# A hybrid stream-encoder layer: token tiles 0 to 3 transposed by TensorE instead of by DMA, their loads and the f weights' issued earlier

## The chip, the cores and the metric

The kernel runs on one core of a Trainium2 chip. The core has five engines with an instruction queue each: TensorE (PE; its weight loads are shown apart as PEld), VectorE (DVE), ScalarE (ACT), GpSimd (POOL) and SyncE (SP), which here issues nearly all DMAs. The metric is the device time of one execution in microseconds (us), less is better.

## The reference, cut to what matters

The input x has 2048 tokens of 1024 channels in float32. One layer is computed:

```python
h = _rmsnorm(x, pre_norm_g[l])
proj = jnp.einsum('btd,de->bte', h, w_in[l])
q_a, f_a, i_a, g_a, u_b, g_b, q_c, k_c, v_c, g_c, f_c = jnp.split(proj, IN_SPLIT_POINTS, axis=-1)
...
o_a = _hgrn2_chunkwise(jax.nn.silu(q_a).reshape(hshape), k_a.reshape(hshape),
                       i_a.reshape(B, T, HGRN_HEADS, HGRN_VAL_DIM), log_f_a.reshape(hshape))
...
pooled = _multiscale_pool(u_b)
...
o_c = _forgetting_attention(q_c.reshape(fshape), k_c.reshape(fshape), v_c.reshape(fshape), log_f_c)
...
mixed = jnp.concatenate([o_a, o_b, o_c], axis=-1)
y = jnp.einsum('bte,ed->btd', mixed, w_out[l])
x = x + _rmsnorm(y, post_norm_g[l])
```

A is a gated linear recurrence (4 heads, 64x64 state; its inputs are q_a, f_a and i_a, 256 columns of the projection each), B a pooling mixer, C a forgetting attention with 8 heads. The input projection has 3592 columns over a depth of 1024.

## The kernel before

**Tiles.** The tokens are cut into 16 tiles of 128 (partitions), and these into 4 groups of 512. Every factor of the projection is split into two float16 halves, high and low, and a product takes three matmuls (high with high, low with high, high with low). The normalised tokens are kept transposed, channels on the partitions: hTh and hTl, high and low halves, 8 blocks of 128 channels.

**A token tile** is made by `x_parts` (L208), a generator which its caller advances with `next`: the load xt (SP), a Square with a sum on ACT (L213), mean and epsilon into ss on DVE (L214), the power -1/2 on POOL (L217, "pow" below), xh on ACT (L218, the tile scaled by ss, as float16), xl on DVE (L220, what xh leaves over), and two DMA transposes on SP, xh into hTh (L221) and xl into hTl (L223). xt, ss, xh and xl have two buffers each.

**Weights** come through `w_parts` (L138): 256 columns in four quarters of two depth blocks, a load into a staging tile wst (three buffers; the weights for i are staged in four others), and for each block a high half wh (L161 on ACT, for i on POOL) and a low half wl (L164 on DVE). The eight columns of the attention's gate stand in wfc (L482 to L484) and are projected together with i.

**The start phase** (L465 to L509) is written out by hand, and `sp()` keeps its instructions in program order (`ordered[0]`, until L509): the loads of tile 0, of the weights for i and of tile 1, tiles 0 to 3 with the halves of i between them, the quarters of f, and the i projection of tiles 0 and 1 (`tok_i`, L235: pi on TensorE, evicted by ACT into va, L239, and fcs, L240). Behind it the library's scheduler chooses each engine's order from what is recorded. Next in the program come the weights q, tiles 4 and 5, and the constants on POOL (masks, d0, zeros; L538 to L583), which `tc.issue_after` puts behind the pow of tile 5. Then the first `hgrn_f` and `hgrn_q` (the projections pf and pq over a group of 512 tokens, and the elementwise work behind them: E, z, b, khat, qhat), the weights k, tiles 6 and 7, and the loads of x8 and x9. The later tiles are fed in between the levels of the recurrence's units (`feed`); there each level makes an X (POOL or DVE, then ACT) and a Z, and TensorE multiplies them; khT (L335) is a transposed khat that pu (L368) needs.

**The rest** is eight such units (4 groups, 2 channel halves), then the projections of the other parts, the attention over blocks of 128 queries, and the output projection.

Of the kernel before, what the change touches and what calls it, by code (L numbers as in the profile page):

```python
# [10 lines left out]
F16 = mybir.dt.float16  # L11
# [4 lines left out]
AF = mybir.ActivationFunctionType  # L16
ALU = mybir.AluOpType
# [5 lines left out]
P = 128  # L23
NT = T // P
KC = D // P
# [29 lines left out]
def kernel(  # L55
# [7 lines left out]
    V, S, G, PE = nc.vector, nc.scalar, nc.gpsimd, nc.tensor  # L63
# [6 lines left out]
    cp = ctx.enter_context(tc.tile_pool(name="cp", bufs=1))  # L70
# [5 lines left out]

    idf = cp.tile([P, P], F32, tag="idf", name="idf")
    make_identity(nc, idf)
    cneg = cp.tile([P, 8], F32, tag="cneg", name="cneg")
    G.memset(cneg, -0.5)  # L80

# [27 lines left out]
    psA = phP.enter_context(tc.tile_pool(name="psA", bufs=1, space=PSUM, reuse_waits="tile"))  # L109
# [7 lines left out]
    def h_at(t0, n):  # L117
        i, o = divmod(t0, T // 2)
        return hTs[i][0][:, :, o:o + n], hTs[i][1][:, :, o:o + n]
# [9 lines left out]
    def sp(ins):  # L129

        if ordered[0]:
            tc.keep_in_program_order(ins)
        return ins
# [3 lines left out]
    def w_parts(segs, name, pool=None, hi_eng=None, stage=None, extra=0):  # L137
        n = sum(w for _, w in segs)  # L138
        pool = pool or wpool
        wh = pool.tile([P, KC, n + extra], F16, tag="wh", name=f"wh_{name}")  # L140
        wl = pool.tile([P, KC, n + extra], F16, tag="wl", name=f"wl_{name}")
        staged = {}

        def load(q):
            if stage:
                st = stage(f"wst_{name}_{q}").rearrange("p (k n) -> p k n", k=WK)
            else:
                st = wpool.tile([P, WK, n], F32, tag="wst", name=f"wst_{name}_{q}", bufs=3)
            o = 0
            for c0, w in segs:  # L150
                sp(nc.sync.dma_start(st[:, :, o:o + w],
                                     win[q * WK * P:(q + 1) * WK * P, c0:c0 + w].rearrange("(k p) c -> p k c", p=P)))
                o += w
            staged[q] = st

        def halves(q):
            st = staged.pop(q)
            for kk in range(WK):
                k = q * WK + kk
                if hi_eng is None:  # L160
                    sp(S.activation(wh[:, k, :n], st[:, kk, :], AF.Copy, bias=0.0, scale=g256[:, k:k + 1]))  # L161
                else:
                    sp(hi_eng.tensor_scalar(wh[:, k, :n], st[:, kk, :], g256[:, k:k + 1], 1.0, op0=ALU.mult, op1=ALU.mult))
                sp(V.scalar_tensor_tensor(wl[:, k, :n], st[:, kk, :], g256[:, k:k + 1], wh[:, k, :n],  # L164
                                          op0=ALU.mult, op1=ALU.subtract))

        return (wh, wl), load, halves
# [28 lines left out]

    last_pow = [None]

    xts = {}
    def x_dma(xpool, t, tag="xt"):  # L200
        xt = (xpool if tag == "xt" else ap).tile([P, D], F32, tag=tag, name=f"xt{t}", bufs=2)
        sp(nc.sync.dma_start(xt, xf[t * P:(t + 1) * P, :]))
        xts[t] = xt

    def x_parts(xpool, t, tag="xt"):
        if t not in xts:
            x_dma(xpool, t, tag)
        xt = xts.pop(t)  # L208
        ss = xpool.tile([P, 4], F32, tag="ss", name=f"ss{t}", bufs=2)
        xh = xpool.tile([P, D], F16, tag="xh", name=f"xh{t}", bufs=2)  # L210
        xl = xpool.tile([P, D], F16, tag="xl", name=f"xl{t}", bufs=2)
        hh, hl = h_at(t * P, P)
        sp(S.activation(xh.bitcast(BF16), xt, AF.Square, bias=0.0, scale=1.0, accum_out=ss[:, 0:1]))  # L213
        sp(V.tensor_scalar(ss[:, 1:2], ss[:, 0:1], 1.0 / (D * SH * SH), EPS / (SH * SH),  # L214
                           op0=ALU.mult, op1=ALU.add))
        yield
        last_pow[0] = sp(G.tensor_tensor(ss[:, 2:3], ss[:, 1:2], cneg[:, 0:1], op=ALU.pow))  # L217
        sp(S.activation(xh, xt, AF.Copy, bias=0.0, scale=ss[:, 2:3]))  # L218
        yield
        sp(V.scalar_tensor_tensor(xl, xt, ss[:, 2:3], xh, op0=ALU.mult, op1=ALU.subtract))  # L220
        sp(nc.sync.dma_start_transpose(hh, xh))  # L221
        yield
        sp(nc.sync.dma_start_transpose(hl, xl))  # L223

    def x_load(xpool, t, tag="xt"):
        for _ in x_parts(xpool, t, tag):
            pass
# [7 lines left out]
    def tok_i(t, wi, va):  # L235
        tt = t % 4
        pi = pj(f"pi{t}")
        proj_tm(pi[:, :264], wi, 0, 264, t)
        sp(S.activation(va[:, tt, :], pi[:, :256], AF.Copy, bias=0.0, scale=INV))  # L239
        sp(S.activation(fcs[:, t, :], pi[:, 256:264], AF.Copy, bias=0.0, scale=INV))  # L240
# [217 lines left out]
    xpool = xstk.enter_context(tc.tile_pool(name="xpool", bufs=2, side="right", reuse_waits="tile"))  # L458
# [7 lines left out]
    wi, load, halves = w_parts([(IA, 256)], "i", hi_eng=G, stage=tmp, extra=8)  # L466
# [3 lines left out]
    wfc = t512("X", "wfc", 4)[:, :8 * KC].rearrange("p (k c) -> p k c", k=KC)  # L470
    sp(nc.sync.dma_start(wfc, win[:, FC:FC + 8].rearrange("(k p) c -> p k c", p=P)))
    x_dma(xpool, 1, "at")
    x0, x1, x2, x3 = (x_parts(xpool, t) for t in range(4))
    next(x0)
    next(x0)
    halves(0)
    next(x0)
    x_dma(xpool, 2, "at")
    next(x0, None)
    x_dma(xpool, 3)  # L480
    halves(1)
    sp(V.tensor_tensor(wfc, wfc, g256.unsqueeze(2).to_broadcast([P, KC, 8]), op=ALU.mult))  # L482
    sp(V.tensor_copy(wi[0][:, :, 256:264], wfc))
# [2 lines left out]
    halves(2)  # L486
    halves(3)
    next(x1)
    next(x1)
    next(x1, None)  # L490
    wf, load, halves = w_parts([(FA, 256)], "f")
    next(x2)
    next(x2)
    next(x2)
    next(x2, None)
    for q in range(3):
        load(q)
    tok_i(0, wi, toks[0])
    next(x3)
    next(x3)  # L500
    next(x3)
    next(x3, None)
# [55 lines left out]
    G.affine_select(out=mdiag, in_=mdiag, pattern=[[1, P]], compare_op=ALU.is_ge,  # L558
                    fill=0.0, base=0, channel_multiplier=-1)

    idh = cp.tile([P, P], F16, tag="idh", name="idh")
    V.tensor_copy(idh, idf)
    idb = cp.tile([P, P], BF16, tag="idb", name="idb")
    V.tensor_copy(idb, idf)

# [30 lines left out]
    def feed():  # L596

        for t in range(8, NT):
            parts = x_parts(xpool, t)
            for k in range(3):  # L600
                next(parts)
                if k < 2:
                    yield
            next(parts, None)
            if t + 2 < NT:
                x_dma(xpool, t + 2)
            yield
# [595 lines left out]
```

## Time and profile before

| | |
|---|---|
| runs | 1254.1, 1251.9, 1248.07 us; median 1251.9 |
| the profiled execution | 1248.18 us, of which the span that the trace shows is 1246.4 |
| granted TensorE clock, mean | 0.987 |
| TensorE matmul / weight load busy | 1170.5 us (94%) / 749.9 (60%) |
| DVE / ACT / POOL busy | 812.2 (65%) / 609.5 (49%) / 403.7 (32%) |
| DMA | 107.56 MB, mean 86 GB/s |

How to read a row of the profile. A row of the timeline has the start in us, the duration, the engine, the line, the operation, the tile written and those read (buffer numbers are left out, so xh is the xh of any token tile), the shape of output and input, and, in brackets, the idle time of that engine just before and what ended it. x2 or x4 behind it means so many in a row, with the time of all. A row of the windows has the stretch, its length, then busy time and count of PE, PEld, DVE, ACT and POOL, then the granted clock, the DMA share and GB/s. The 40 slices show busy tenths in equal parts of the span (31 us each).

### The profile page before, as it was taken

The page shows a single profiled execution, that of the slowest core. Times are in us where ns is not written, and L with a number is a line of the kernel's source. Part 1 is how long each engine was busy: PE and PEld are TensorE (multiplying, and loading weights), DVE is VectorE, ACT ScalarE, POOL GpSimd, SP SyncE. Part 2 cuts the span into 40 slices and gives each one's busy share as a digit, 9 for nine tenths or more (in the row PEclk, how much of TensorE's full clock was granted, in tenths as well). Part 3 has the DMA queues.
Part 4 walks back from the last instruction along what each step waited for, and adds up shares of the span by engine and source line. Part 5 has one row for each costly group of instructions (what it writes and reads, how often), then busy time and mean ns, then how long its engine had stood idle before and what let it go on. Part 6 is the DMA issues. An engine that isn't in the chain of part 4 may idle for free.

```text
span 1246.4 us, 25487 instructions
## 1 busy us (share of the span) xinstructions
PE 1170.5 (94%) x9949; PEld 749.9 (60%) x9949; DVE 812.2 (65%) x1736; ACT 609.5 (49%) x1176; POOL 403.7 (32%) x500
## 2 busy tenths in 40 slices
PE   5877999999999999999999999999989899999998
PEld 3445667655644588884447767755555555555544
DVE  5787878887433243214364799788788888888522
ACT  5756444553121222212122677667767676777611
POOL 2645555553130020002230223234334343434400
PEclk9988999999999999999999999999999999999999
DMA  9646100113175232101112343285223222321263
GB/s 226 184 115 170 44 17 18 52 35 93 43 183 142 71 107 71 35 2 43 26 51 70 89 140 110 69 178 127 67 64 85 68 78 79 65 51 38 80 162 104
DMA packets 168137, 107.56 MB, mean 86 GB/s; under 512 B 95824, under 2 KB 159568, under 8 KB 168016
## 3 DMA queue, kind: packets, MB, share of 16 engines
q1 hardware_dynamic: 166976, 105.92, 32.2%
q8 instruction: 78, 1.28, 0.4%
q14 instruction: 43, 0.35, 0.1%
q10 hardware_dynamic: 1040, 0.00, 0.0%
HBM read 59.62 MB, written 31.59 MB: 73 GB/s over the span
## 4 chain that ended last, share of the span: by engine, by line
PE 62%; DVE 19%; ACT 6%; issue 5%; POOL 4%; DMA 4%; SPq 0%; POOLq 0%; DVEq 0%; ACTq 0%
PE y L1078 11%; PE pq L183 7%; PE pv L194 6%; PE pgc L194 5%; PE pu L183 3%; PE st L1009 3%; PE st L1010 3%; PE pgb L183 3%; PE pk L183 3%; DVE pl L1024 3%; PE mx L973 3%; DVE M L979 3%; PE o L1034 2%; PE o L1035 2%; PE pf L183 2%
## 5 line engine op out<-in xcount | busy, mean ns | idle before, releaser
L1019 ACT ACTIVATE pf<-st,biasg 128x512 f32<-128x512 f32 (+1 forms) x320 | 199.6, 625 | 93.9 <-PE st L1010 53.2
L194 PEld LDWEIGHTS <-hTh 128*128 128x128 f16 x1536 | 151.0, 99 | 44.3 <-DMA hTh<-xh 16.1
L1024 DVE TENSOR_TENSOR pl<-pf,ph 128x512 f16<-128x512 f32 (+1 forms) x213 | 139.9, 658 | 42.4 <-POOL ph L1021 24.8
L1024 POOL TENSOR_TENSOR pl<-pf,ph 128x512 f16<-128x512 f32 (+2 forms) x107 | 114.2, 1067 | 147.7 <-ACT ph L1023 137.6
L979 DVE TENSOR_REDUCE M<-mx 128x1 f32<-128x512 f32 x192 | 129.2, 682 | 9.4 <-PE mx L973 8.5
L1023 ACT ACTIVATE ph<-st,biasg 128x512 f16<-128x512 f32 (+2 forms) x213 | 131.4, 617 | 2.1 <-PE o L1036 2.1
L1034 PE MATMUL o<-Vt,ph 128*128 128x65 f16 x1088 | 129.7, 193 | 2.8 <-DVE oc L1048 2.4
L1035 PE MATMUL o<-Vt,ph 128*128 128x64 f16 x1088 | 130.2, 195 | 0.0
L1036 PE MATMUL o<-Vt,pl 128*128 128x65 f16 x1088 | 129.2, 192 | 0.0
L1021 POOL TENSOR_SCALAR ph<-pf 128x512 f16<-128x512 f32 (+1 forms) x107 | 66.0, 617 | 192.4 <-ACT pf L1019 130.8
L1034 PEld LDWEIGHTS <-ph 128*128 128x128 f16 x1088 | 102.6, 96 | 34.5 <-issue 5.5
L1009 PE MATMUL st<-QQ,K 128*128 128x512 f16 (+1 forms) x320 | 111.5, 349 | 5.6 <-ACT ph L1023 5.0
L1035 PEld LDWEIGHTS <-ph 128*128 128x128 f16 x1088 | 101.8, 97 | 24.5 <-issue 1.1
L1036 PEld LDWEIGHTS <-pl 128*128 128x128 f16 x1088 | 102.3, 99 | 0.4
L1078 PE MATMUL y<-woh,mh 128*128 128x512 f16 (+2 forms) x264 | 98.2, 373 | 0.0
L1078 PE MATMUL y<-woh,ml 128*128 128x512 f16 (+2 forms) x264 | 98.0, 373 | 0.0
L1078 PE MATMUL y<-wol,mh 128*128 128x512 f16 (+2 forms) x264 | 98.0, 373 | 0.0
L973 PE MATMUL mx<-KA,QM 68*128 68x512 f16 (+1 forms) x224 | 79.5, 358 | 5.7 <-DVE M L979 4.1
L194 PEld LDWEIGHTS <-hTl 128*128 128x128 f16 x768 | 75.5, 98 | 9.9
L1010 PE MATMUL st<-QB,KA 68*128 68x512 f16 x224 | 80.1, 358 | 0.0
L1078 PEld LDWEIGHTS <-mh 128*128 128x128 f16 x528 | 49.4, 98 | 50.4 <-issue 0.7
L976 DVE CUSTOM_DVE_ANT_0 mx<-mx,negq 128x128 f32<-128x128 f32 (+3 forms) x128 | 62.3, 492 | 12.0 <-PE mx L973 11.5
(327 smaller groups left out, 2691.1 us busy)
## 6 DMA issues: line engine op xcount, KB each, us to landing
xt<-in_x_dram SPq DMA_DIRECT2D x16, 512.0 KB, 4.4
xr<-in_x_dram SPq DMA_DIRECT2D x16, 512.0 KB, 4.5
out_dram<-yt SPq DMA_DIRECT2D x15, 512.0 KB, 3.1
QQ<-qh_d SPq DMA_DIRECT2D x64, 64.0 KB, 2.3
wo<-in_w_out_dram SPq DMA_DIRECT2D x16, 256.0 KB, 3.0
gc_d<-gtc SPq DMA_DIRECT2D x32, 128.0 KB, 2.0
gtl<-gc_d SPq DMA_DIRECT2D x16, 256.0 KB, 2.9
wst_q<-in_w_in_dram SPq DMA_DIRECT2D x12, 256.0 KB, 2.9
```

What stands on the lines that cost most here:

```text
L183: PE.matmul(ps, a[:, k, c0:c0 + P], b[:, k, :], start=i == 0, stop=i == 3 * KC - 1)
L194: PE.matmul(ps, a[:, k, :], b[:, k, c0:c0 + n], start=i == 0, stop=i == 3 * KC - 1)
L979: V.tensor_reduce(dst, mx[:, :w], op=ALU.max, axis=AX.X)
L1009: PE.matmul(st[:, off:], K2[c][:, h, jj * P:(jj + 1) * P], QQs[i][:, off:], start=True, stop=False)
L1010: PE.matmul(st[:, off:], KA[c][:68, h, jj * P:(jj + 1) * P], QBs[i][:68, off:], start=False, stop=not diag)
L1019: S.activation(pf[:, off:], st[:, off:], AF.Exp, bias=bias, scale=0.125)
L1023: S.activation(ph[:, off:], st[:, off:], AF.Exp, bias=bias, scale=0.125)
L1024: (G if k == 1 else V).tensor_tensor(pl[:, off:], pf[:, off:], ph[:, off:], op=ALU.subtract)
L1034: PE.matmul(pov[:, qi, :], ph[:, qs], Vt[:, j, h, 0:65], start=(j == 0 and qi == 0), stop=False, skip_group_check=True)
L1035: PE.matmul(pov[:, qi, 0:64], ph[:, qs], Vt[:, j, h, 65:129], start=False, stop=False, skip_group_check=True)
L1036: PE.matmul(pov[:, qi, :], pl[:, qs], Vt[:, j, h, 0:65], start=False, stop=(j == 4 * g + qi), skip_group_check=True)
L1078: PE.matmul(py, a[:, k, :], b[:, k, cs], start=i == 0, stop=i == 3 * KC - 1)
```

## The change

An identity in float16, idh, is made at the very start instead of behind the constants. For tiles 0 to 3 `x_parts` makes no DMA transposes any more: `pe_transposed` has TensorE transpose the eight 128x128 blocks of xh into a PSUM bank (tag pm, one of six), and ACT copies them into hTh; xl goes the same way, and DVE copies it into hTl. These tiles now take one `next` less. The loads of x2 and x3 and of the first three f quarters stand further ahead in the program.

```diff
+    idh = cp.tile([P, P], F16, tag="idh", name="idh")
+    V.tensor_copy(idh, idf)
...
+    def pe_transposed(src, name):
+        pt = psA.tile([P, KC, P], F16, tag="pm", name=name, bufs=6)
+        for k in range(KC):
+            PE.transpose(pt[:, k, :], src[:, k * P:(k + 1) * P], idh)
+        return pt
...
         last_pow[0] = sp(G.tensor_tensor(ss[:, 2:3], ss[:, 1:2], cneg[:, 0:1], op=ALU.pow))
         sp(S.activation(xh, xt, AF.Copy, bias=0.0, scale=ss[:, 2:3]))
+        if t < 4:
+
+            sp(S.activation(hh, pe_transposed(xh, f"xhT{t}"), AF.Copy, bias=0.0, scale=1.0))
+            yield
+            sp(V.scalar_tensor_tensor(xl, xt, ss[:, 2:3], xh, op0=ALU.mult, op1=ALU.subtract))
+            sp(V.tensor_copy(hl, pe_transposed(xl, f"xlT{t}")))
+            return
         yield
...
     x_dma(xpool, 1, "at")
+    x_dma(xpool, 2, "at")
+    x_dma(xpool, 3)
     x0, x1, x2, x3 = (x_parts(xpool, t) for t in range(4))
     next(x0)
     next(x0)
     halves(0)
-    next(x0)
-    x_dma(xpool, 2, "at")
     next(x0, None)
-    x_dma(xpool, 3)
     halves(1)
...
     halves(3)
     next(x1)
-    next(x1)
     next(x1, None)
     wf, load, halves = w_parts([(FA, 256)], "f")
-    next(x2)
+    for q in range(3):
+        load(q)
     next(x2)
     next(x2)
     next(x2, None)
-    for q in range(3):
-        load(q)
     tok_i(0, wi, toks[0])
-    next(x3)
     next(x3)
     next(x3)
     next(x3, None)
...
-    idh = cp.tile([P, P], F16, tag="idh", name="idh")
-    V.tensor_copy(idh, idf)
```

The order of the engines' rows before the first unit and in it is another one; further on the rows of ACT, DVE, POOL, SP and TensorE are the same again. TensorE has 128 rows more (64 transposes and their weight loads), ACT and DVE four each, SP eight fewer. In the rows that follow, a number behind a name tells buffers apart; names like xh6 carry the token tile.

DVE before, behind xl of tile 0 (L164 are low halves of i, L482 to L484 the gate columns, L214 the ss of tile 1):

```order
L220 SCALAR_TENSOR_TENSOR xl0_129<-xt0_111,ss0_127,xh0_128 128x1024
L164 SCALAR_TENSOR_TENSOR wl_i_114<-wst_i_1_117,g256_69,wh_i_113 128x256 x2
L482 TENSOR_TENSOR wfc_123<-wfc_123,g256_69 128x64
L516 TENSOR_TENSOR lb_e_326<-lbt_324 128x2
L483 CAST wh_i_113<-wfc_123 128x8x8
L484 TENSOR_TENSOR wl_i_114<-wfc_123,wh_i_113 128x8x8
L214 TENSOR_SCALAR ss1_152<-ss1_152 128x1
```

DVE of the change at the same place:

```order
L231 SCALAR_TENSOR_TENSOR xl0_135<-xt0_113,ss0_133,xh0_134 128x1024
L232 COPY hTl0_100<-xlT0_155 128x8x128
L166 SCALAR_TENSOR_TENSOR wl_i_116<-wst_i_1_119,g256_71,wh_i_115 128x256 x2
L496 TENSOR_TENSOR wfc_125<-wfc_125,g256_71 128x64
L497 CAST wh_i_115<-wfc_125 128x8x8
L498 TENSOR_TENSOR wl_i_116<-wfc_125,wh_i_115 128x8x8
L222 TENSOR_SCALAR ss1_172<-ss1_172 128x1
```

The copy of xlT0 out of PSUM now stands between xl0 and all that follows it.

ACT before, from the q halves (wh_q) to the first elementwise row of hgrn_f (E):

```order
L161 ACTIVATE wh_q_341<-wst_q_1_349,g256_69 128x256 x2
L213 ACTIVATE xh5_382,ss5_381<-xt5_379 128x1024
L218 ACTIVATE xh5_382<-xt5_379,ss5_381 128x1024
L161 ACTIVATE wh_q_341<-wst_q_2_355,g256_69 128x256 x2
L161 ACTIVATE wh_q_341<-wst_q_3_361,g256_69 128x256 x2
L254 ACTIVATE E_0_0_486<-pf_0_0_460 128x512
```

ACT of the change, from the Square of tile 5 (L221) to the same row:

```order
L221 ACTIVATE xh5_456,ss5_455<-xt5_453 128x1024
L221 ACTIVATE xh6_651,ss6_650<-xt6_648 128x1024
L163 ACTIVATE wh_f_208<-wst_f_3_303,g256_71 128x256 x2
L254 ACTIVATE va0_112<-pi3_371 128x256
L255 ACTIVATE fcs_74<-pi3_371 128x8
L163 ACTIVATE wh_q_415<-wst_q_0_417,g256_71 128x256 x2
L163 ACTIVATE wh_q_415<-wst_q_1_423,g256_71 128x256 x2
L226 ACTIVATE xh5_456<-xt5_453,ss5_455 128x1024
L226 ACTIVATE xh6_651<-xt6_648,ss6_650 128x1024
L163 ACTIVATE wh_q_415<-wst_q_2_429,g256_71 128x256 x2
L163 ACTIVATE wh_q_415<-wst_q_3_435,g256_71 128x256 x2
L269 ACTIVATE E_0_0_558<-pf_0_0_532 128x512
```

The Squares of tiles 5 and 6 have moved ahead of the last f halves, and xh of tile 6 (L226) ahead of the last q halves. On POOL the pow of tile 6, which xh6 needs, stands behind the constants, before and now.

ACT before, in the first unit (khat L287, X of two levels L350, E and z of the second channel half):

```order
L287 ACTIVATE khat_0_0_509<-khat_0_0_509 128x512
L350 ACTIVATE X_0_0_64_729<-X_0_0_64_729 128x512
L350 ACTIVATE X_0_0_32_746<-X_0_0_32_746 128x512
L254 ACTIVATE E_0_1_774<-pf_0_1_604 128x512
L255 ACTIVATE z_0_1_773<-pf_0_1_604 128x512
```

ACT of the change there:

```order
L365 ACTIVATE X_0_0_64_801<-X_0_0_64_801 128x512
L221 ACTIVATE xh8_814,ss8_813<-xt8_660 128x1024
L226 ACTIVATE xh7_665<-xt7_662,ss7_664 128x1024
L365 ACTIVATE X_0_0_32_818<-X_0_0_32_818 128x512
L226 ACTIVATE xh8_814<-xt8_660,ss8_813 128x1024
L269 ACTIVATE E_0_1_846<-pf_0_1_676 128x512
```

The xh of tiles 7 and 8 now stand on both sides of the X of level 32; before, they came later.

## The prediction

> **What bounds the kernel now.** I read the page first: the span, the busy shares, the 40 slices and the shares of the chain that ended last.
>
> ```profile
> span 1246.4 us, 25487 instructions
> PE 1170.5 (94%) x9949; PEld 749.9 (60%) x9949; DVE 812.2 (65%) x1736; ACT 609.5 (49%) x1176; POOL 403.7 (32%) x500
> PE   5877999999999999999999999999989899999998
> PE 62%; DVE 19%; ACT 6%; issue 5%; POOL 4%; DMA 4%; SPq 0%; POOLq 0%; DVEq 0%; ACTq 0%
> ```
>
> A slice is 31 us. From the sixth on TensorE is full, so a shift at the start reaches the end nearly whole; only in the first five (155 us) do other engines set the pace. The change lies in the first 30 us of these. Next come the stretches (busy time of PE, PEld, DVE, ACT, POOL, each with its count):
>
> ```profile
> 20.00:25.00 5.00, 2.59 (x13) 1.65 (x12) 1.44 (x2) 2.51 (x4) 0.55 (x1) 0.76 1.06 276
> 60.00:70.00 10.00, 4.15 (x40) 3.39 (x38) 7.03 (x14) 6.42 (x14) 2.76 (x3) 0.85 0.37 105
> ```
>
> and the tile hTh: what its readers waited for, and its transposes from issue to landing.
>
> ```profile
>   DMA hTh<-xh: 19.2, 6
> DMA to landing us min/median/max: 2.7/3.3/5.1
> ```
>
> TensorE does wait for hTh, 19.2 us in six waits. But at 20 to 25 us all engines are half idle and nothing after them is ready either: what counts is when the x tiles, the f halves and the q halves are done, in the order of ACT's, DVE's and POOL's queues.
>
> **The change part by part.** It removes eight DMA transposes (hTh and hTl of tiles 0 to 3), adds 64 TensorE transposes, four ACT evictions (L229 of the change) and four DVE copies (L232), and moves loads forward. The timeline of before, from which I take every duration (start, us, instruction, idle time and its releaser):
>
> ```profile
> 6.68 1.15 ACT L218 ACTIVATE xh<-xt,ss 128x1024 f16<-128x1024 f32 x1 [0.93 <-POOL ss L217]
> 8.39 1.49 DVE L220 SCALAR_TENSOR_TENSOR xl<-xt,ss,xh 128x1024 f16<-128x1024 f32 x1
> 9.81 1.31 DVE L164 SCALAR_TENSOR_TENSOR wl_i<-wst_i,g,wh_i 128x256 f16<-128x256 f32 x2
> 11.78 0.38 PE L194 MATMUL pi<-wh_i,hTh 128*128 128x264 f16 x1 [11.78 <-DVE wh_i L483]
> 11.97 0.14 DVE L214 TENSOR_SCALAR ss<-ss 128x1 f32<-128x1 f32 x1
> 12.28 0.42 PE L194 MATMUL pi<-wh_i,hTh 128*128 128x264 f16 x1
> 12.50 0.42 PE L194 MATMUL pi<-wl_i,hTh 128*128 128x264 f16 x1
> 12.97 1.15 ACT L218 ACTIVATE xh<-xt,ss 128x1024 f16<-128x1024 f32 x1 [1.20 <-POOL ss L217]
> 14.04 1.06 ACT L213 ACTIVATE xh<-xt 128x1024 bf16<-128x1024 f32 x1
> 16.24 1.15 ACT L218 ACTIVATE xh<-xt,ss 128x1024 f16<-128x1024 f32 x1 [1.05 <-POOL ss L217]
> 17.48 0.36 ACT L239 ACTIVATE va<-pi 128x256 f32<-128x256 f32 x1
> 19.13 1.06 PE L194 MATMUL pi<-wh_i,hTl 128*128 128x264 f16 x8
> 25.64 1.69 ACT L161 ACTIVATE wh_f<-wst_f,g 128x256 f16<-128x256 f32 x4
> ```
>
> Step 1, tile 0. DVE's copy of xlT0 stands ahead of the second pair of wl_i, of wfc and of tile 1's ss. It waits for eight transposes after xl0 (ended 9.88). A transpose streams 128 columns; 264 take 0.22 us from start to start at 12.28 and 1.06/8 at 19.13, so eight take 0.5 to 0.9. The trace has no copy of 1024 elements out of PSUM: it costs no less than the 0.57 of an eviction of 512 (the ACT row at 41.28 below), no more than the 1.49 at 8.39. I take 1.15, near ACT's 1.15 for 1024, and 1.1 for ACT's own. DVE is then 2.2 us later: ss of tile 1 goes from 11.97 to 14.2, its xh from 12.97 to 15.2, the first pi matmul, which waits for wfc's halves, from 11.78 to 14.0. Both ends of the copy's price move this step by -0.6 or +0.3.
>
> Step 2, tiles 1 to 3. On ACT each tile's eviction now stands between its xh and the next Square, so the tiles run one behind another. A tile's own chain, Square to the end of xh, is 16.24 + 1.15 - 14.04 = 3.35 us. Tile 1: xh ends at 16.35; its transposes stand behind 12 pi matmuls (14.0 + 12 x 0.22 = 16.6) and end by 17.7; eviction to 18.9. Tile 2: 3.35 + 0.6 + 1.1, to 23.95. Then pi's eviction (0.5 with fcs) and tile 3, with the Square of x4 ahead of its xh and the xh of x4 ahead of its eviction: Square at 24.2, xh to 27.7, xh4 to 28.8, eviction to 29.8. The first f half, at 25.64 before, starts at 29.7: 4 us late, although its weights lie ready. The earlier loads of x2, x3 and f0 to f2 buy nothing, for x2 is wanted at 18.8 and was there before at 14.04.
>
> Step 3, f3 and q. wst_f has three buffers, so f3's load waits for the DVE pair on f0, which now stands behind xl4 and the copy of xlT3.
>
> ```profile
> 29.10 1.57 SPq L151 DMA_DIRECT2D wst_f<-in_w_in_dram  x1
> 33.25 0.91 ACT L161 ACTIVATE wh_f<-wst_f,g 128x256 f16<-128x256 f32 x2 [2.26 <-DMA wst_f<-in_w_in_dram]
> 36.63 1.06 ACT L213 ACTIVATE xh<-xt 128x1024 bf16<-128x1024 f32 x1 [0.40 <-DVE wl_q L164]
> 38.04 0.55 POOL L217 TENSOR_TENSOR ss<-ss,cneg 128x1 f32<-128x1 f32 x1 [13.49 <-DVE ss L214]
> 38.54 0.53 POOL L539 MEMSET d<- 128x512 f32 x1
> 38.63 1.15 ACT L218 ACTIVATE xh<-xt,ss 128x1024 f16<-128x1024 f32 x1 [0.85 <-POOL ss L217]
> 39.68 1.69 ACT L161 ACTIVATE wh_q<-wst_q,g 128x256 f16<-128x256 f32 x4
> 41.28 0.57 ACT L254 ACTIVATE E<-pf 128x512 f32<-128x512 f32 x1
> 45.89 0.51 ACT L161 ACTIVATE wh_k<-wst_k,g 128x256 f16<-128x256 f32 x1 [0.68 <-DMA wst_k<-in_w_in_dram]
> 48.12 0.72 POOL L217 TENSOR_TENSOR ss<-ss,cneg 128x1 f32<-128x1 f32 x1
> 50.25 1.22 DVE L271 TENSOR_TENSOR_SCAN b<-d,E 128x512 f32<-128x512 f32 x1
> 52.62 1.13 ACT L218 ACTIVATE xh<-xt,ss 128x1024 f16<-128x1024 f32 x1
> ```
>
> By the same counting DVE frees f0 at 32.1, so f3 moves from 29.10 to 32.1 and its half from 33.25 to 36.3: 3 us. Then the delay shrinks: before, ACT had the Square of x5 at 36.63 between the q halves; now the Squares of x5 and x6 are done at 32.8 to 35.1, while ACT waits for f3. xh5 runs at 39.1 (38.63 before).
>
> Step 4, the new wait. ACT's row behind xh5 is now xh6, ahead of the halves of q2 and q3; before, xh6 ran at 52.62. xh6 needs POOL's pow of tile 6, and on POOL that pow still stands behind the constants. In the trace the constants fill 38.54 to 48.12, 9.6 us, and the pow of tile 5 starts 0.5 ahead of them. The pow of tile 5 moves to 34.3, the constants to 34.8, the pow of tile 6 to 44.4, so xh6 starts at 45.2 and the q halves, 39.68 before, at 46.2: **6.5 us late**. ACT stands idle from 40.3 to 45.2. Queued behind it are q2, q3 and the evictions of pf, so TensorE's pq and the whole elementwise chain of the first unit wait. Bounds: if tiles and POOL come 1 us earlier, 5.5; if the constants, which share their time with more DVE work, stretch by a tenth, 8.5.
>
> Step 5. The load of k's second quarter stands on SP behind the transposes of tile 6 (xl6 only at 48); it issues at 50.2 and lands at 53.4 instead of 45.9. So b starts at 58.3 instead of 50.25: 8.1.
>
> Step 6, the first unit. On ACT xh7 now stands ahead of X of level 32, and its pow on POOL behind qhat; the Square of x9 stands ahead of khT.
>
> ```profile
> 58.09 0.63 ACT L350 ACTIVATE X<-X 128x512 f32<-128x512 f32 x1 [0.40 <-POOL X L349]
> 59.61 2.26 POOL L309 TENSOR_TENSOR qhat<-qhat,qs 128x512 f32<-128x512 f32 x1
> 71.31 2.08 PE L368 MATMUL pu<-va,khT 128*128 128x128 f32 x8 [6.55 <-ACT khT L335]
> ```
>
> And the chain that ended last, in order of time, at one step:
>
> ```profile
> 77.99 4.13 DMA xt<-in_x_dram
> ```
>
> qhat's end, 61.9, becomes 69.9; xh7 ends at 71.5; X of level 32 runs there instead of at 58.09. x9 lands at 78.3, khT ends at 82.2, and pu starts at 82.3 instead of 71.31: 11 us, 3 more than in step 5. From there it gives back: the 4.13 us in which the chain stood on x10's load go, since x10 is issued at 77.6 now, at the old time in a later program: 11.0 - 4.1 = 6.9. Then TensorE's order lets the level 8 to 2 matmuls of the second unit behind 16 pf matmuls; that costs nothing to 16 x 0.22 = 3.5; I take 2.5, nearer to the row. From here the orders are equal.
>
> Sum: 6.5 + 1.6 (step 5) + 2.9 (step 6) - 4.1 + 2.5 = **9.4 us late**, on TensorE's full stretch. The profiled execution took 1248.2 (span 1246.4 and 1.8 around it): 1248.2 + 9.4 = 1257.6. It lies 3.7 below the median of the runs, 1251.9, by which it would be 1261.3. I write 1258. The 128 added TensorE instructions count 2 x 32 x 0.055 to 0.11, 4 to 7 us, but lie in gaps.
>
> Two pages bear on this. The Trainium skill, "Advanced Engine Details and Errata", X-Bar Transpose, says transposing DMAs are as fast as plain ones; the trace agrees so far as it shows them (3.3 us to landing at the median), and by that alone nothing is gained by their going. The Trainium skill, "VectorE: DVE Perf Modes", Rules for kernel authors, says to transpose 128x128 on TensorE where PSUM may receive it; what that would make of the time is the second rival.
>
> **Rivals.** (a) The new wait is absorbed. If xh6 did not stop ACT, the q halves would start right behind xh5, at 39.1 + 1.15 = 40.3, 0.6 late, and the sum would be 0.6 + 1.6 + 2.9 - 4.1 + 2.5 = 3.5: 1252. For it: 6.55 us of TensorE idle at 71.31 and ACT's 49% leave room. Against: order and wait are fixed, and nothing on ACT can pass xh6. It decides if the constants take under 4 us instead of 9.6.
>
> (b) Faster. The waits for hTh (19.2 us in six) end with the DMA, and the free queue brings all loads early. That needs a tile to take hardly more than before. If the evictions cost 0.57 and the transposes hide, tiles take 3.9 each, tile 3 is done by 26, the first f half starts where it did (25.64) and f3 and q, loaded ahead, come 3 earlier than before, and the constants end 4 earlier than I say, so that xh6 hardly stops ACT: 1248.2 - 4 = 1244. This would be the rule of the Trainium skill, "VectorE: DVE Perf Modes", at work. Against: step 1's order delays tile 1 however fast the rest is.
>
> (c) Slower still: the constants and the X of POOL stretch by a tenth or more with DVE busier beside them, and x11's and x12's loads do not gain: 9.4 + 6 = 15, 1263.
>
> That the transposes stay on the DMA can be left out: TensorE's rows show them.
>
> **How the numbers follow.** Forecast 0.54, (c) 0.12, (a) 0.24, (b) 0.10. Some 0.5%, 6 us, is what a measurement of this kernel can tell from no change. Slower takes the forecast and (c): 0.66; the same is (a): 0.24; faster (b): 0.10. The range goes from 1250, near (a), to 1267, (c) by the median of the runs; (b) and the tails left out hold under 2 in 10.
>
> **What would show it.** After: the first f half near 29.7 (step 2); the Square of x5 before f3's half, and ACT idle some 5 us before xh6, released by POOL (step 4); pow of tile 6 near 44.4; b near 58; pu near 82 (step 6). A first f half before 26, or a pow of tile 6 before 41, would make the forecast wrong; so would TensorE less than full between 160 and 1200 us, where a late start could be made up.

## The result and the profile after

The changed kernel takes 1256.88 us (median of 10 runs, 1253.23 to 1259.94) against 1249.93 for the kernel before (10 runs beside it, 1246.38 to 1254.1): ratio **1.0056**, interval 1.004 to 1.0072, or 7.0 us more. Its profiled execution took 1255.51, 7.3 more than the profiled one of before, at a mean granted clock of 0.983 (0.987 before). The page of the changed kernel, in the rows shown of before (span, busy shares, TensorE in 40 slices, shares of the chain that ended last):

```profile
span 1253.8 us, 25612 instructions
PE 1179.8 (94%) x10013; PEld 755.3 (60%) x10013; DVE 814.3 (65%) x1740; ACT 612.1 (49%) x1180; POOL 398.6 (32%) x500
PE   5968899999999999999999999999989899999998
PE 63%; DVE 18%; ACT 5%; POOL 5%; issue 5%; DMA 3%; SPq 0%; POOLq 0%; DVEq 0%; ACTq 0%
```

TensorE is full from the sixth slice on, as before. The time was lost in the first five. The two stretches of before again (busy time and count of PE, PEld, DVE, ACT, POOL, then clock, DMA share, GB/s):

```profile
20.00:25.00 5.00, 4.30 (x45) 3.63 (x46) 2.47 (x6) 4.47 (x12) 0.55 (x1) 1.00 0.34 107
60.00:70.00 10.00, 7.71 (x74) 6.54 (x72) 8.46 (x13) 5.67 (x9) 7.12 (x9) 1.00 0.31 78
```

Taken alone they look like a success. From 20 to 25 us TensorE works 4.30 us where it worked 2.59, and ACT 4.47 where it worked 2.51: the waits for the DMA's transposes are gone. But ACT is busier with tiles, not with what the first unit waits for. That shows in the timeline of the changed kernel, the rows of the prediction's steps in order of time (start, us, instruction, idle time before and its releaser):

```profile
8.84 1.02 ACT L229 ACTIVATE hTh<-xhT 128x1024 f16<-128x1024 f16 x1 [1.13 <-PE xhT L204]
9.82 1.03 PE L204 MATMUL xlT<-idh,xl 128*128 128x128 f16 x8 [1.02 <-DVE xl L231]
10.89 0.69 DVE L232 COPY hTl<-xlT 128x1024 f16<-128x1024 f16 x1 [1.13 <-PE xlT L204]
12.88 0.38 PE L196 MATMUL pi<-wh_i,hTh 128*128 128x264 f16 x1 [2.03 <-DVE wh_i L497]
20.68 0.62 PE L204 MATMUL xhT<-idh,xh 128*128 128x128 f16 x8 [0.72 <-ACT xh L226]
26.83 1.02 ACT L229 ACTIVATE hTh<-xhT 128x1024 f16<-128x1024 f16 x1
27.73 1.70 ACT L163 ACTIVATE wh_f<-wst_f,g 128x256 f16<-128x256 f32 x4
32.20 0.55 POOL L225 TENSOR_TENSOR ss<-ss,cneg 128x1 f32<-128x1 f32 x1 [6.53 <-DVE ss L222]
35.46 0.91 ACT L163 ACTIVATE wh_f<-wst_f,g 128x256 f16<-128x256 f32 x2 [2.49 <-DMA wst_f<-in_w_in_dram]
40.24 0.82 POOL L225 TENSOR_TENSOR ss<-ss,cneg 128x1 f32<-128x1 f32 x1
41.09 1.15 ACT L226 ACTIVATE xh<-xt,ss 128x1024 f16<-128x1024 f32 x1 [1.76 <-POOL ss L225]
42.15 1.69 ACT L163 ACTIVATE wh_q<-wst_q,g 128x256 f16<-128x256 f32 x4
43.55 2.65 SPq L238 DMA_TRANSPOSE hTl<-xl  x2
46.30 1.05 SPq L153 DMA_DIRECT2D wst_k<-in_w_in_dram  x2
50.93 0.91 ACT L163 ACTIVATE wh_k<-wst_k,g 128x256 f16<-128x256 f32 x2 [4.29 <-DMA wst_k<-in_w_in_dram]
55.10 1.22 DVE L286 TENSOR_TENSOR_SCAN b<-d,E 128x512 f32<-128x512 f32 x1
64.45 1.45 POOL L324 TENSOR_TENSOR qhat<-qhat,qs 128x512 f32<-128x512 f32 x1
66.63 1.15 ACT L226 ACTIVATE xh<-xt,ss 128x1024 f16<-128x1024 f32 x1 [3.07 <-POOL ss L225]
67.69 0.61 ACT L365 ACTIVATE X<-X 128x512 f32<-128x512 f32 x1
78.95 2.08 PE L383 MATMUL pu<-va,khT 128*128 128x128 f32 x8 [7.16 <-ACT khT L350]
```

Read it as a ladder against the rows of before: the first f half is 2.1 us late, the last q halves 2.5, k's second quarter 5.0 (50.93 against 45.89), b 4.9, the X of level 32 9.6, pu 7.6. The profiled execution ends 7.3 late: what TensorE had lost when pu of the first unit started, it never got back. On ACT three waits mark the rungs: 1.76 us for POOL at xh6, 4.29 for the load of k, which stood on SP behind tile 6's transposes, and 3.07 for POOL at xh7.

### The profile page after: what moved, and what is told of

Its sections match the earlier page's. It is cut to its first block, busy times and chain, and to the rows that moved or that the text cites. A ratio compares the mean times of both kernels' runs of the same rounds, so it can differ in the third digit from the quotient of the medians.

```text
span 1253.8 us, 25612 instructions
## 1 busy us (share of the span) xinstructions
PE 1179.8 (94%) x10013; PEld 755.3 (60%) x10013; DVE 814.3 (65%) x1740; ACT 612.1 (49%) x1180; POOL 398.6 (32%) x500
## 4 chain that ended last, share of the span: by engine, by line
PE 63%; DVE 18%; ACT 5%; POOL 5%; issue 5%; DMA 3%; SPq 0%; POOLq 0%; DVEq 0%; ACTq 0%
PE y L1087 11%; PE pq L185 7%; PE pv L196 6%; PE pgc L196 5%; PE st L1018 3%; PE pu L185 3%; PE st L1019 3%; PE pgb L185 3%; PE pk L185 3%; PE mx L982 3%; DVE pl L1033 3%; DVE M L988 3%; PE pi L196 2%; PE o L1043 2%; PE o L1044 2%
```

## The experiments

**Theories.** T1, that of the prediction: tiles 6 and 7 (and the late f halves, behind tiles 1 to 3) now stand ahead of the first unit's work in the queues of ACT, POOL and SP. T2: TensorE's transposes and their evictions cost the time themselves. T3: one wait, that of xh6 for the constants on POOL, is the price. In what follows "held" means a scheduling edge (`tc.issue_after`): the work is placed behind the named instruction. Each job ran the kernel before beside its kernels, 18 to 23 times, with medians of 1249.21 to 1250.4 us.

Starts from the one profiled execution of each, in us, and the timed ratio (where a start lies inside a group of rows, it is worked out from the group's start and the distance of its rows, 0.40 us between two halves):

| | before | changed | e1 | e2 | e3 | e5 | e6 | e7 | e9 | e10 | e11 | e12 |
|---|---|---|---|---|---|---|---|---|---|---|---|---|
| first f half | 25.64 | 27.73 | 24.00 | 27.94 | 27.89 | 27.92 | 27.31 | 23.05 | 22.93 | 18.54 | 28.04 | 18.36 |
| f3's half, the last | 33.25 | 35.46 | 32.90 | 36.02 | 35.65 | 35.63 | 35.03 | 30.14 | 32.35 | 30.34 | 35.81 | 30.00 |
| k's second quarter | 45.89 | 50.93 | 45.30 | 45.64 | 49.82 | 47.36 | 46.37 | 42.44 | 44.27 | 43.10 | 46.40 | 42.16 |
| b | 50.25 | 55.10 | 54.95 | 51.14 | 53.99 | 53.51 | 52.90 | 47.99 | 49.81 | 50.39 | 51.64 | 48.66 |
| X of level 32 | 58.09 | 67.69 | 68.29 | 63.35 | 66.58 | 65.89 | 61.53 | 55.82 | 58.73 | 58.23 | 60.27 | 62.28 |
| pu, first unit | 71.31 | 78.95 | 77.26 | 75.29 | 77.99 | 77.52 | 75.03 | 69.72 | 71.41 | 72.13 | 73.78 | 72.62 |
| pu, third unit | 151.71 | 159.43 | 158.44 | 156.60 | 159.27 | 159.56 | 158.37 | 152.60 | 152.85 | 153.36 | 155.78 | 152.51 |
| ratio to before | 1 | 1.0056 | 1.0038 | 1.0013 | 1.006 | 1.0093 | 1.0031 | 1.0009 | 1.0004 | 0.9983 | 1.0023 | 1.0013 |

The intervals of the ratios reach 0.001 to 0.002 to each side, so a difference of two kernels below some 2 us (0.0016, from two intervals of 0.0011) is not clear of noise.

### e1: the loads alone, without any transpose on TensorE

```diff
 (the kernel before)
     x_dma(xpool, 1, "at")
+    x_dma(xpool, 2, "at")
+    x_dma(xpool, 3)
...
     wf, load, halves = w_parts([(FA, 256)], "f")
+    for q in range(3):
+        load(q)
     next(x2)
...
-    for q in range(3):
-        load(q)
     tok_i(0, wi, toks[0])
```

> Only the loads are moved forward; tiles 0 to 3 are transposed by DMA as before. Queue theory (the loss comes from what tiles 6 to 8 put in front of the first unit on ACT, POOL and SP): xh6 stays behind the q halves, so little of the loss is here: between -1 and +3 us against before, the first f half within 1 us of 25.6. Load theory (the early loads pull tile 6 forward and that alone costs): +5 to +8 us. Tile theory (TensorE's transposes and their evictions delay f): 0, within 2 us.

Measured: 1254.31 us, 1.0038 (1.0025 to 1.0052), 4.8 us late. The transposes stay on the DMA, and most of the loss is there all the same. ACT's timeline of e1, the xh of tiles 6 and 7 and the X of level 32:

```profile
50.58 1.15 ACT L218 ACTIVATE xh<-xt,ss 128x1024 f16<-128x1024 f32 x1 [2.58 <-POOL ss L217]
66.20 1.15 ACT L218 ACTIVATE xh<-xt,ss 128x1024 f16<-128x1024 f32 x1 [2.32 <-POOL ss L217]
68.29 0.61 ACT L350 ACTIVATE X<-X 128x512 f32<-128x512 f32 x1
```

The f half (24.00) and k's second quarter (45.30) are early here. Then xh6 stands inside the elementwise chain of the first unit and waits 2.58 us for POOL, so b is 4.7 late, and xh7 does it again ahead of the X. That is T1's mechanism without T2's. The forecast of the queue theory, -1 to +3, was missed all the same: xh6 did stay behind the q halves, but the chain to b, in which it now stood, had been left out. The load theory's sentence, that the early loads pull tile 6 forward and that alone costs, is what happened, at 4.8 where it had +5 to +8.

### e2, e6, e7: tile 6 held behind the first unit's Qd

e2 holds the whole of tile 6 behind Qd, one of the first unit's last rows on ACT before the levels:

```diff
 (the changed kernel)
-        S.activation(q_d, lfo, AF.Exp, bias=0.0, scale=1.0)
+        held[0] = S.activation(q_d, lfo, AF.Exp, bias=0.0, scale=1.0)
...
-    x_load(xpool, 6)
+    with tc.issue_after(held[0].ins):
+        x_load(xpool, 6)
```

> The changed kernel, but on ACT the Square and xh of tile 6 are put behind Qd of the first unit, near where xh6 stood before. Queue theory: the q halves no longer wait for POOL and k's second quarter loads ahead of tile 6's transposes, so b starts near 52 instead of 55.1, and the total falls by 2 to 4 us against the changed kernel, to +3 to +5 us against before. Tile theory: nothing changes, +6 to +8 us against before.

Measured: 1250.72 us, 1.0013 (1.0002 to 1.0023), 1.6 us late: 5.4 of the 7 are gone, more than the 2 to 4 that were expected, and all the new work on TensorE, ACT and DVE is still there. ACT's timeline of e2, a later quarter of k, now with hardly a wait, and xh6:

```profile
46.83 0.91 ACT L163 ACTIVATE wh_k<-wst_k,g 128x256 f16<-128x256 f32 x2 [0.28 <-DMA wst_k<-in_w_in_dram]
62.30 1.15 ACT L227 ACTIVATE xh<-xt,ss 128x1024 f16<-128x1024 f32 x1 [3.73 <-POOL ss L226]
```

xh6 still makes ACT wait, now ahead of the X of level 32; b is 0.9 late instead of 4.9. (The profiled execution took 1255.02, above the median by 4.3, so its trace shows less of the gain than the timed runs.)

e6 lets tile 6's load and Square go early and holds only its xh and what follows:

```diff
 (the changed kernel, with held[0] as in e2)
-    x_load(xpool, 6)
+    x6 = x_parts(xpool, 6)
+    next(x6)
+    with tc.issue_after(held[0].ins):
+        for _ in x6:
+            pass
```

> The changed kernel, but only xh of tile 6 is put behind Qd of the first unit on ACT, where it stood before; its Square and its pow stay early. Queue theory: no wait of ACT for POOL at xh6 (3.73 us in the run with Square and xh held), X of level 32 right behind X of level 64 as before, b near 51, pu at 73 to 75 instead of 78.95; total -1 to +2 us against before. Tile theory: +6 to +8 us; the f half is as late as in the changed kernel (27.7 to 28).

Measured: 1254.2 us, 1.0031 (1.0018 to 1.0043; one run of 2443 us is left out of the ratio), 3.9 us late, between the forecasts of the two theories. The first unit's X comes at 61.53 and pu at 75.03, 3.9 earlier than in the changed kernel; but the third unit's pu is late again, at 158.37. In between the chain that ended last goes over the loads of three token tiles, in e6:

```profile
77.74 4.55 DMA xt<-in_x_dram
100.84 4.21 DMA xt<-in_x_dram
107.46 4.87 DMA xt<-in_x_dram
```

By the third unit's pu, 2.9 of the 3.9 us that the first unit had gained are gone again. The three waits for loads sum to 13.6 us, where the changed kernel's chain has two that sum to 10.4 (shown further down); that they are what took the gain is read from the chain and not tested.

e7 is e1 with the edit of e6 (the transposes on the DMA, loads early, xh6 held).

> Loads moved forward with DMA transposes, and xh of tile 6 behind Qd. Queue theory: the 4.8 us that the loads alone cost go, since they were ACT's wait at xh6 (2.58 us for POOL and 1.15 for xh6 itself ahead of the chain to b) and the same at xh7; with f half and q halves 1 us early, total -3 to +1 us against before. If the cost of the loads is anything else (queues of the DMA, the loads beside each other), +3 to +6 us stay.

Measured: 1251.05 us, 1.0009 (0.9998 to 1.0021). That is 1.1 us late, at the upper end of the queue theory's forecast. The edit of e6 is worth 3.6 us on top of e1 (0.0038 - 0.0009, times 1250) and 3.1 on top of the changed kernel (0.0056 - 0.0031).

### e3, e4: the wait on the constants alone

e3 lets the constants on POOL go behind the pow of tile 4 instead of tile 5, so that they are over before xh6 needs its pow:

```diff
 (the changed kernel)
+    pow4 = last_pow[0]
...
-    constants.enter_context(tc.issue_after(last_pow[0].ins))
+    constants.enter_context(tc.issue_after(pow4.ins))
```

> The changed kernel, but the constants may stand on POOL from the pow of tile 4 on instead of tile 5, so POOL starts them some 6 us earlier and the pow of tile 6 is not behind them when xh6 needs it; the rest of the order is nearly that of the changed kernel. Queue theory: no wait of ACT for POOL at xh6 (1.76 us in the changed kernel), total 1 to 4 us below the changed kernel, +3 to +6 us against before. Tile theory: +6 to +8 us.

Measured: 1257.43 us, 1.006 (1.0046 to 1.0073): nothing gained. ACT's timeline of e3: xh5 and xh6, the q halves, k's second quarter, xh7, and the X of level 32.

```profile
38.38 2.17 ACT L226 ACTIVATE xh<-xt,ss 128x1024 f16<-128x1024 f32 x2
40.46 0.90 ACT L163 ACTIVATE wh_q<-wst_q,g 128x256 f16<-128x256 f32 x2
49.82 0.91 ACT L163 ACTIVATE wh_k<-wst_k,g 128x256 f16<-128x256 f32 x2 [4.07 <-DMA wst_k<-in_w_in_dram]
65.52 1.15 ACT L226 ACTIVATE xh<-xt,ss 128x1024 f16<-128x1024 f32 x1 [3.06 <-POOL ss L225]
66.58 0.61 ACT L365 ACTIVATE X<-X 128x512 f32<-128x512 f32 x1
```

The wait before xh6 is gone (xh5 and xh6 run as one pair), and the next q halves start 1.7 us earlier than in the changed kernel, the last pair of them 0.9 earlier. But k's load still waits on SP behind tile 6's transposes, and ACT waits 4.07 us for it instead of 4.29. b and the first unit's pu come 1.1 and 1.0 us earlier, the third unit's pu 0.2, and the timed runs not at all. **T3 falls**, and with it the forecast of the queue theory (+3 to +6; 7.5 measured, in the tile theory's range). The wait that I had priced highest is not what the time hangs on.

e4 adds to e3 an edge that was to free the X of level 32 from the wait at xh7:

```diff
 (e3)
+    pow7 = last_pow[0]
...
-            E1.tensor_tensor(Xv[:, :, 0, :], mid, nbv[:, :, 0, :], op=ALU.add)
+            with tc.issue_after(pow7.ins) if (g, ct, h) == (0, 0, 32) else ExitStack():
+                E1.tensor_tensor(Xv[:, :, 0, :], mid, nbv[:, :, 0, :], op=ALU.add)
```

> As the run with the earlier constants, and the pow of tile 7 is put ahead of the second half of X of level 32 on POOL, so that xh7, and X of level 32 behind it on ACT, do not wait for qhat (3.07 us in the changed kernel). Queue theory: 1.5 to 3 us less than with the earlier constants alone, +1.5 to +4 us against before, the rest being the f half that is 2.1 us late. Tile theory: +6 to +8 us.

Measured: 1252.9 us, 1.0029 (1.0017 to 1.004). That is 3.6 us late, inside the queue theory's forecast, but the cause can't be read from it: in the trace the edge put half of that X behind qhat and behind the pow at 65.12 us, the wait at xh7 was still 2.03 us, the third unit's pu came at 159.94, and the profiled execution (1258.98) lies 6 us above the median. Inconclusive.

### e5: k's load ahead of tile 6's transposes on SP

```diff
 (the changed kernel)
-                sp(nc.sync.dma_start(st[:, :, o:o + w],
+                wdma[name, q] = sp(nc.sync.dma_start(st[:, :, o:o + w],
...
-    x_load(xpool, 6)
+    x_dma(xpool, 6)
+    with tc.issue_after(wdma["k0", 1].ins):
+        x_load(xpool, 6)
...
-    x_load(xpool, 7)
+    with tc.issue_after(wdma["k0", 1].ins):
+        x_load(xpool, 7)
```

> The changed kernel, with one thing moved: on SP the two transposes of tile 6 (and tile 7's load) are put behind the load of k's second quarter; ACT keeps xh6 ahead of the last q halves. Queue theory, with SP as its main part: that load issues near 44.5 us instead of 46.3 and lands 47 to 48.5 instead of 50.9, b of the first unit starts at 52 to 53.5 instead of 55.1, total 1 to 3 us below the changed kernel (+4 to +6 us against before). If ACT's and POOL's order is the main part: no more than 1 us below the changed kernel. Tile theory (late f half alone): +6 to +8 us.

Measured: 1262.23 us, 1.0093 (1.008 to 1.0107), the slowest of all. Rows of e5's timeline: on SP the load of k and, now behind it, two transposes; k's second quarter and xh7 on ACT; and TensorE much later.

```profile
44.54 1.16 SPq L153 DMA_DIRECT2D wst_k<-in_w_in_dram  x2
45.75 1.23 SPq L237 DMA_TRANSPOSE hTh<-xh  x1
47.03 1.52 SPq L239 DMA_TRANSPOSE hTl<-xl  x1
47.36 1.55 ACT L163 ACTIVATE wh_k<-wst_k,g 128x256 f16<-128x256 f32 x3 [0.56 <-DMA wst_k<-in_w_in_dram]
64.31 1.15 ACT L227 ACTIVATE xh<-xt,ss 128x1024 f16<-128x1024 f32 x1 [4.13 <-POOL ss L226]
663.74 0.37 PE L196 MATMUL pgc<-wh_gc,hTh 128*128 128x256 f16 x1 [4.08 <-DVE mb L880]
668.73 0.27 PE L196 MATMUL pgc<-wh_gc,hTh 128*128 128x256 f16 x1
```

The rung it aimed at went as wanted: k's second quarter 3.6 us earlier. The wait at xh7 grew from 3.07 to 4.13, b gained 1.6, pu 1.4, and the third unit nothing (159.56 against 159.43). What it loses beyond the change (4.6 us by the ratios) has another place: at 663.74 TensorE stood 4.08 us for DVE's mb, and then ran at half speed to 668.73 (its matmuls start 0.21 us apart, later 0.11). In the changed kernel the first 24 of these pgc matmuls run ahead of that wait, from 658.99 on, and it is 1.47 us long; in e5 none does. That is far from the edit and I did not find what ties the two; so e5 shows that this link alone gains nothing in the first three units, and its total of 11.6 us, outside every forecast, is not a price of SP's order.

### e8: the transposes twice

```diff
 (the changed kernel)
-        for k in range(KC):
+        for k in [*range(KC), *range(KC)]:
```

> The changed kernel with each of the 64 TensorE transposes done twice into the same place; the orders of all other engines are the same row for row. If the transposes lie in gaps, as the prediction has it: within 1.5 us of the changed kernel, +5.5 to +8.5 us against before. If they stand on the tile chain: eight more transposes cost 0.5 to 1.0 us per half and tile, the first f half moves from 27.7 to 30 or later, and the total is +9 to +12 us against before.

Measured: 1260.05 us, 1.0068 (1.0049 to 1.0087). The order of the other engines is that of the changed kernel. The intervals of e8 and of the change overlap, and the difference of the ratios is 0.0012, 1.5 us; pu of the first unit comes at 79.67 against 78.95, pu of the third at 160.71 against 159.43. So 64 more transposes cost about a microsecond, at the upper end of the first forecast, and the 64 of the change are not likely to be the 7. They don't lie wholly in gaps, though: the first f half starts at 29.43, 1.7 later than in the changed kernel, and most of it is then swallowed, since ACT's wait at xh6 shrinks from 1.76 to 0.41. The evictions by ACT and DVE were not doubled. **T2 falls** by e2 and by e10 below, where all transposes and evictions stay and most or all of the loss is gone.

### e9, e10: all tiles held; the transposes on the DMA or on TensorE

The scheduler pulls later tiles forward too. e9 is e7 with tiles 12 to 15 held behind the third unit's Qd:

```diff
 (e7)
-        S.activation(q_d, lfo, AF.Exp, bias=0.0, scale=1.0)
+        qds[(g, ct)] = S.activation(q_d, lfo, AF.Exp, bias=0.0, scale=1.0)
...
-                next(parts)
+                with tc.issue_after(qds[(1, 0)].ins) if t >= 12 else ExitStack():
+                    next(parts)
```

> As the run with the loads alone and xh6 behind Qd, and from tile 12 on the token tiles stand behind the third unit's Qd on ACT, so that their Squares and xh, which wait for loads, are not in the middle of that unit's chain. Queue theory: the first unit keeps its lead (pu near 69.7), the second no longer gives it back (second pu near 113 instead of 116.6), total -3.5 to -0.5 us against before. If what the second unit loses is set by the loads of x themselves or by DVE: second pu at 116 or later, total 0 to +2.5 us.

e10 is the changed kernel (transposes on TensorE) with the same holds on xh6 and on tiles 12 to 15, and with the first f half and f3's load ahead of tile 2's xh:

```diff
 (the changed kernel, with the edits of e6 and e9)
     next(x2)
+    halves(0)
+    load(3)
...
-    halves(0)
-    load(3)
```

> The changed kernel with its transposes, and three things moved: the first f half and f3's load stand ahead of tile 2's xh, xh of tile 6 behind the first unit's Qd, tiles 12 and later behind the third unit's Qd. Queue theory: the transposes and their evictions cost nothing that reaches the end once the queues are in order; f3's half at 32 to 33.5 instead of 35.46, b near 50, total -1.5 to +2 us against before. Tile theory (the evictions on ACT and DVE are the loss): +4 to +7 us.

Measured in one job: e9 1251.18 us, 1.0004 (0.9993 to 1.0016), the same as before; e10 **1248.61 us, 0.9983 (0.9972 to 0.9994)**. e9 missed the queue theory's forecast: its second pu, at 115.15, lies between the 113 and the 116 of the two, and the first, at 71.41, lost the lead that e7 had (69.72). By the ratios e10 is 2.1 us below the kernel before, a little more than the queue theory had, and 9.1 below the changed kernel. It has the same transposes and evictions as the change; only the order is another one. Its timeline, first f half, xh6, X of level 32 and pu:

```profile
18.54 0.89 ACT L163 ACTIVATE wh_f<-wst_f,g 128x256 f16<-128x256 f32 x2
52.76 1.14 ACT L227 ACTIVATE xh<-xt,ss 128x1024 f16<-128x1024 f32 x1
58.23 0.63 ACT L366 ACTIVATE X<-X 128x512 f32<-128x512 f32 x1 [0.41 <-POOL X L365]
72.13 2.07 PE L384 MATMUL pu<-va,khT 128*128 128x128 f32 x8 [6.44 <-ACT khT L351]
```

xh6 has no wait before it, and the X of level 32 runs at 58.23 (58.09 in the kernel before). The start is not faster than before, however: the third unit's pu comes 1.7 us later than there. What makes e10's total the smaller one arises behind it (see what stays open).

### e11, e12: the early f half, taken apart

e11 is e10 without the move of the f half.

> The changed kernel with xh of tile 6 behind the first unit's Qd and tiles 12 and later behind the third unit's Qd; the f halves stay where the change has them, behind tile 3's eviction. Against the run that has the early f half as well (-2.1 us against before): if the late f half is a loss of its own once ACT's order behind it is clean, 1.5 to 4 us more, that is -0.5 to +2 us against before; if the order of tiles 6 and 12 was all, no difference, -3 to -1 us.

Measured: 1253.24 us, 1.0023 (1.0012 to 1.0034), 2.9 us late, a little above the range for a late f half. So the move of one f half and one load is worth 5.0 us (0.0023 + 0.0017, times 1250; give or take 2, and from two jobs) where the tiles are held already. In the traces 2.4 of it stand at the third unit's pu (155.78 against 153.36). The move does more than undo the lateness: f3's half starts at 30.34 in e10, 5.5 earlier than in e11 and 2.9 earlier than in the kernel before.

e12 is the changed kernel with that move alone.

> The changed kernel, only the first f half and f3's load moved ahead of tile 2's xh; the tiles from 6 on stay where the scheduler puts them. Tile theory: the whole loss was the f half, total -2 to +2 us against before. Queue theory: f3's half at 32 to 33.5 instead of 35.46 but ACT still waits at xh6 or xh7 for POOL, total +3 to +6 us against before.

Measured: 1251.46 us, 1.0013 (1.0003 to 1.0023): 5.4 us better than the change, and 1.6 late, which is the range that I had given to the tile theory (the whole loss was the f half). ACT's timeline of e12, first f half, xh6, and xh7:

```profile
18.36 0.89 ACT L163 ACTIVATE wh_f<-wst_f,g 128x256 f16<-128x256 f32 x2
42.96 1.13 ACT L226 ACTIVATE xh<-xt,ss 128x1024 f16<-128x1024 f32 x1
60.19 1.15 ACT L226 ACTIVATE xh<-xt,ss 128x1024 f16<-128x1024 f32 x1 [3.54 <-POOL ss L225]
```

With f early, the scheduler also placed xh6 behind k's second quarter (42.16), where its pow is ready. So e12 mixes the two causes and can't tell them apart; e11 against e10 is the cleaner price of the f weights' place. The wait at xh7 is still there, 3.54 us, ahead of the X of level 32.

**Together.** Along one path: the change +7.0; xh6 held (e6) -3.1; tiles 12 to 15 held (e11) -1.0; f early (e10) -5.0; end at -2.1. The step of 1.0 is not clear of noise. These are steps of that path and not prices that add in any order: e2 and e12, each with one edit, take away 5.4. That the order of the queues is the loss is shown, since e10 has all the work of the change; how the loss divides between tile 6 and the f weights is not.

## Why the prediction was right, and where it was not

**The direction and the place were right, and the size was near, in part by luck.** It said 9.4 us late from the first unit, carried through by a full TensorE; it came 7.3 late in the profiled execution, with 7.6 at the first unit's pu and 7.7 at the third's. The 1258 lies within 1.1 us of the 1256.88 only because it was counted from a profiled execution of 1248.2, which is 1.7 below the median of before (1249.93). And one of the prediction's own signs against itself came true: a pow of tile 6 before 41 was to make the forecast wrong, and it started at 40.24. The time still came late because, as e3 shows, it did not hang on that pow. Rival (b) is out: the waits for hTh did end, and nothing was gained. Rival (c) is out, the constants were shorter and not longer. Rival (a), 3.5 us, is out too: it wanted constants under 4 us, they took 7.5, and the wait was there; but the q halves' delay of 2.5 lies nearer to its 0.6 than to the forecast's 6.5. e3 tests its condition: without the wait the kernel is 7.5 late and not 3.5.

**Point by point.**

- Step 1, tile 0: the first pi matmul went from 11.78 to 12.88, 1.1 late against 2.2. The order was as said. The copy took 0.69 us, not 1.15, and the pair of wl_i behind it 0.87 us instead of 1.31. ACT's eviction of 1.02 met the 1.1, and eight transposes, at 0.61 to 1.06, went a little above the 0.5 to 0.9.
- Step 2, tiles 1 to 3: f half at 27.73, forecast 29.7. The order was right (xh3 and xh4 ahead of the last eviction, which runs at 26.83); the 1.1 from step 1 and some 0.3 a tile were too much.
- Step 3: f3's half 2.2 late, forecast 3. The step then let this delay shrink to half a microsecond at xh5 and gave the late f weights no term of their own. e11 and e10 say otherwise: with the tiles held, moving them is worth 5.0 us, though part of that is a start earlier than before.
- Step 4, the new wait: **the mis-sized term.** ACT stood 1.76 us, not 5, and the q halves came 2.5 late, not 6.5. Tile 5's pow came 2.1 us ahead of the forecast (32.20 against 34.3), and the constants took 7.5 us, not 9.6. In the windows of the same 31 POOL instructions, before and then changed (DVE is the third busy time, ACT the fourth, POOL the fifth):

```profile
38.50:48.10 9.60, 8.50 (x39) 3.57 (x38) 7.70 (x13) 8.79 (x18) 9.60 (x31) 1.00 0.85 222
```

```profile
32.70:40.20 7.50, 7.11 (x36) 3.46 (x34) 3.88 (x8) 4.14 (x11) 7.50 (x31) 0.94 0.74 182
```

  POOL's time for the same work fell by a fifth where DVE's share fell from 80% to 52% and ACT's from 92% to 55%. I had allowed for a stretch by a tenth and not for a shrinking. That DVE's or ACT's work is what stretches POOL's is argued from these two rows, not shown.
- Step 4 as a cause: e3 took this wait away and gained nothing. The step named the right tile and the wrong part of it. What costs is the order as a whole: e2, which moves tile 6 with its xh on ACT and its transposes on SP, takes away 5.4, and so does e12, which moves the f weights and, by the scheduler, xh6.
- Step 5: k's load did stand behind tile 6's transposes. b lost 2.4 more there (from 2.5 to 4.9), against 1.6. e5 and e6 bring the load forward, by other means, and b follows by 1.6 and 2.2.
- Step 6: xh7 did stop ACT ahead of the X of level 32, by 3.07 us, and pu lost 2.8 more than b, against 2.9. This term had the right size.
- The give-back was wrong: the 4.1 us of x10's load were to go. The chain that ended last in the changed kernel stands on two token loads as the one of before did, and for longer (before 4.13 at 77.99 and 4.13 at 99.70):

```profile
70.44 4.63 DMA xt<-in_x_dram
102.65 5.76 DMA xt<-in_x_dram
```

  Between the first and the third unit's pu nothing came back (+7.6, then +7.7). What the level 8 to 2 matmuls cost behind pf, forecast 2.5, can't be told apart in this. Nor are the orders equal from there on, as the prediction took it: the two programs still differ on POOL in the places of the pows of tiles 13 to 15, and on ACT and DVE in those of the fourth unit's elementwise rows.

So two errors worked against each other, and that the sum came within 2 us is luck: the wait was 4 too large, and a give-back of 4.1 less 2.5 did not come. In the terms as measured the sum is 2.5 + 2.4 + 2.8 - 0.3 = 7.4, where the last is from pu to the end of the span.

Of the two pages that the prediction named, "VectorE: DVE Perf Modes" in the Trainium skill, Rules for kernel authors, prefers TensorE for a transpose of 128x128. The runs agree only under a condition: as the change places it, it costs 7.0 us; with the orders put right on both sides, the transposes on TensorE (e10, 0.9983) are 0.0021 or 2.6 us (give or take 2) ahead of those on the DMA (e9, 1.0004). That lead is not earned where the transposes stand, since e10's first and third pu start later than e9's; and the two differ in the place of the f weights as well.

**What stays open.** Why e10 is ahead of e9: the starts of its first and third unit (72.13, 153.36) are not earlier than e9's (71.41, 152.85). The traces show where the lead arises: behind the third unit TensorE waits 1.4 us for DVE's Vt and 1.2 for gtb in e9 (1.3 and 1.2 in the kernel before), and in e10 0.2 for Vt, nothing for gtb and 0.6 more for gtc. What ties these waits to the transposes is not shown. Why the profiled executions of e2, e4 and e6 lie 1 to 6 us above their medians. What ties e5's edit to the wait at 663.74 us. And the changed transposes with the loads in their old places were not run: the program that comes out has every engine's instructions in the order of the changed kernel, so on top of the transposes the move of the loads should alter nothing.

## What to carry to other kernels

When a slow step at the start is made faster, look at what the scheduler puts into the time that comes free: here later token tiles slid ahead of the first unit in three in-order queues, and cost 7 us, while the waits for the slow step had gone. Removing one wait of such a chain gained nothing here (e3, e5), since the next one took its place; hold the early work as a whole behind the urgent chain (e2), and put the urgent weights first (e12). And price a change on the engine that waits by the next thing in its queue, not by the idle time that it removes.

## What the runs showed of the hardware

- Speed of TensorE after a wait. In e5 the matmuls take 0.42 us each from 663.74 on, after 4.08 us of idling, and 0.27 from 668.73 on, 5.0 us later; in the changed kernel a wait of 1.47 us for the same tile left them at 0.28. The Trainium skill, "TensorE: Matmul & The Clock Gate", Part 1, has a window of about 3.4 us: at least one of them idle for half speed, at least one busy for full speed again; the 4.08, the 1.47 and the 5.0 agree.
- The granted clock of a stretch does not show all of it: the changed kernel's window from 5 to 20 us has a clock of 1.00 (the number behind POOL's busy time), while its pi matmuls start 0.22 us apart up to 16.33 and 0.11 apart from 16.54 on.

```profile
5.00:20.00 15.00, 9.15 (x70) 7.09 (x70) 9.93 (x28) 7.78 (x12) 6.77 (x11) 1.00 0.84 287
```

- A DMA transpose keeps SP longer than most loads. In the first 70 us of the kernel before, the medians on SP are 1.23 us for a transpose into hTh, 0.37 for a load of k and 0.56 for one of x. In e5's rows above single transposes take 1.23 and 1.52 us, two loads of k together 1.16. In the changed kernel k's second quarter stands behind four transposes, two of them tile 6's.
